# A causal mask added by VectorE with the row maximum, and mLSTM scores from three products of rounded halves

## The chip, the cores and the metric

One Trainium2 chip, one of its cores. The metric is the device time of one execution in microseconds (us); below are the times of three runs and the profile of one execution. PE is TensorE (matmuls; PEld is its weight load), DVE is VectorE, ACT is ScalarE, POOL is GpSimd, SP issues most DMAs.

## What is computed

A decoder of two layers over 256 tokens, width 2048, all in float32: an mLSTM layer with a gated ConvFFN, then a layer of differential attention with a gated ConvFFN, each on a residual stream, and a final RMSNorm. The change touches two places of it.

```python
# mLSTM, per head: scores of queries and keys, times a causal decay weight
s = jnp.einsum('bhtd,bhsd->bhts', qb, kb) * jnp.exp(dmat - m_t[..., None])
num = ... + jnp.einsum('bhts,bhsv->bhtv', s, vb)
...
# attention, per head and per each of its two score maps
s = jnp.einsum('bqhcd,bkhcd->bhcqk', qb, kb)
mask = (start + jnp.arange(Q_BLOCK))[:, None] >= jnp.arange(end)[None, :]
p = jax.nn.softmax(jnp.where(mask, s, -jnp.inf), axis=-1)
pd = p[:, :, 0] - lam * p[:, :, 1]
```

There are 8 heads in both; an mLSTM head has 128 query and key dimensions, an attention head two maps of 128.

## The kernel before

Weights stream from memory in tiles of 1 MB (`raw`, 4 buffers). `granule` takes half a tile and splits it for TensorE: ACT copies it, rounded to the format float32r, into a `w2` buffer (L376), and DVE puts what the rounding left beside it (L377). There are 5 `w2` buffers (`HL`). A matmul of two float32 operands is then three matmuls of halves, high by high, low by high and high by low. A matmul whose operands are plain float32 is run by TensorE as two instructions.

The mLSTM layer goes through q (`first_product`), the gates, k (`gemm`), v and the output gate o. For v and o (`gemm_tokens`, L437; four groups of 512 columns each) a granule is two of the 16 slices of the contraction, or 12 matmuls with 512 columns. In the two middle groups of o, `gemm_sevenths` (L503, L493) takes slices 8 to 11 in another way: `sevenths` loads one tile, DVE makes differences of its blocks (L449 to L451), and four `w2` buffers are filled from these (L458, L459). Their products go partly into the group's accumulators (`acc`), partly into two banks `mix`. A `w2` buffer comes free when the last product that reads it is done. The small PSUM banks (`small_ps`, 4 in all) are shared by `mix`, the scores, `val_ps`, `cols_ps` and others.

Work of a head is queued with `later(n, ...)`, to be written n granules on. When the two heads of a v group are ready, `weights(h)` forms the exponent of the decay in bank `w_ps` (L778), DVE adds the mask `mask_s` (L780), ACT takes the exponential (L782 to L784), PE the scores into `s_ps` (L786: 256 queries by the first 128 keys, L787: the last 128 by the last 128), DVE multiplies (L788), and the product is split (`split_weights`, L321, L323). Two granules later `values` multiplies it with v (`val_ps`, L335), squares (L343) and, later, `scaled` writes `hn` (L348). The heads' results are used when o's groups end (L819, L820, transposed at L357).

In attention, `halves(h)` splits keys and late queries into `kh, kl, qh, ql`. `softmax(h)` then forms, for each of the two maps, a bank `as_ps` with 384 columns: 256 for the later queries (L987, three products) and 128 for the first ones (L988, plain float32). One bfloat16 product of an identity with `mask_a` (L989) adds -1e30 above the diagonal. DVE takes the row maxima from the bank (L991, two a map), ACT the exponentials from the bank into `pc` (L996).

The order in which each engine gets its instructions is not that of the code: the framework (`schedule_with_timeline_sim`) places them by a timeline of its own, apart from `first_product`. Buffers of a pool are given out in that process too.

Of the kernel before, what the change touches and what calls it, by code (L numbers as in the profile page):

```python
# [10 lines left out]
F32 = mybir.dt.float32  # L11
F32R = mybir.dt.float32r
BF16 = mybir.dt.bfloat16
I32 = mybir.dt.int32
AF = mybir.ActivationFunctionType
ALU = mybir.AluOpType
AX = mybir.AxisListType
PSUM = bass.MemoryType.PSUM

P = 128  # L20
D = 2048
T = 256
# [11 lines left out]
SCALE = QK ** -0.5  # L34
LAMBDA_INIT = 0.8 - 0.6 * math.exp(-0.3)
NEG = -1e30
G = 512
NG = D // G
RAW = 4
# [29 lines left out]
def trunk(  # L69
# [6 lines left out]
    nc = tc.nc  # L76
    act, dve, pool, pe = nc.scalar, nc.vector, nc.gpsimd, nc.tensor

    const = ctx.enter_context(tc.tile_pool(name="const", bufs=1))
# [7 lines left out]
    def block(dt, name, width=T):  # L87

        b = big.tile([P, 2 * T + 4], dt, tag="block", name=name)
        return b[:, :width], b[:, width:2 * width], b[:, :2 * width]  # L90

    def tmp(name, rows=P, dt=F32):
        return work.tile([rows, T], dt, tag="tmp", name=name, bufs=8)

    def small_ps(name):
        return sm_ps.tile([P, 512], F32, tag="sm", name=name)
# [17 lines left out]
    def later(granules, fn):  # L114
        clock[1] += 1
        heapq.heappush(waiting, (clock[0] + granules, clock[1], fn))
# [21 lines left out]
    dve.tensor_copy(ident_r, ident)  # L138
    both_r = const.tile([P, HEADS], F32R, name="both_r")
    dve.tensor_tensor(both_r, ident[:, :HEADS], ident[:, 32:32 + HEADS], op=ALU.add)  # L140
    ident_b = const.tile([P, P], BF16, name="ident_b")
    make_identity(nc, ident_b)
    ones = const.tile([P, P], F32, name="ones")
    pool.memset(ones, 1.0)
    half_pi = const.tile([P, 1], F32, name="half_pi")
# [1 line left out]

    mask_a = const.tile([P, 2 * P], BF16, name="mask_a")
    mask_s = const.tile([P, 2 * P], BF16, name="mask_s")
    for m, sign in ((mask_a, 1), (mask_s, -1)):  # L150
        pool.memset(m, 0.0)
        m = m.rearrange("p (a c) -> p a c", a=2)
        pool.affine_select(out=m, in_=m, pattern=[[0, 2], [-sign, P]], compare_op=ALU.is_ge, fill=NEG, base=0, channel_multiplier=sign)

    def rows_of(ap):
        return ap.rearrange("(r c) -> r c", c=P)
# [55 lines left out]
    class Norm:  # L212
# [9 lines left out]
        def squares(self, g):  # L222
            for t in range(2):
                act.activation(tmp("sq").bitcast(BF16), stream[:, t, g * G:(g + 1) * G], AF.Square, accum_out=self.parts[:, t, g:g + 1])

# [78 lines left out]
    def scaled_split(ps, scale, name, width=T):  # L304
        h, l, hl = block(F32R, name, width)
        act.activation(h[:, :T], ps, AF.Identity, scale=scale)
        dve.scalar_tensor_tensor(l[:, :T], ps, scale, h[:, :T].bitcast(F32), op0=ALU.mult, op1=ALU.subtract)
        return h, l, hl
# [112 lines left out]

    def gemm_tokens(xs, w, col0, groups, evac, cw=G, lead=1):

        kn, hc = len(xs), WCOLS // cw // 2
        order, last = in_order(kn, hc, groups, lead, held=4 // hc)
        raws, accs = {}, {}
        for j, k0 in order:
            if k0 == 0:
                accs[j] = [acc_ps.tile([P, 2 * T], F32, tag="acc", name="acc")[:, :cw] for _ in range(2)]
            ps = accs[j]  # L430
            for i, (wh, wl) in enumerate(granule(w, col0 + j * cw, cw, k0, kn, raws, j)):
                k = k0 + i
                xh, xl, _ = xs[k]
                for t in range(2):
                    s = slice(t * P, (t + 1) * P)
                    for o, (a, b) in enumerate(((xh, wh), (xl, wh), (xh, wl))):
                        pe.matmul(ps[t], a[:, s], b, start=(k == 0 and o == 0), stop=(k == kn - 1 and o == 2))  # L437
            if k0 == last:
                evac(j, accs.pop(j))
            tick()  # L440

    def sevenths(w, c0, k0, n):


        raw = wpool.tile([P, 4, G], F32, tag="raw", name="raw", bufs=RAW)[:, :2 * n]
        loads.append(nc.sync.dma_start(raw, w[k0 * P:(k0 + 2 * n) * P, c0:c0 + G].rearrange("(k p) n -> p k n", p=P)))
        b = raw.rearrange("p (a k) (c n) -> p a (k c) n", a=n, c=2)
# [16 lines left out]
    def gemm_sevenths(xs, mixed, w, col0, groups, evac, at):  # L464
# [3 lines left out]
        for g in groups:  # L468
# [3 lines left out]
            while k0 < kn:  # L472
                if k0 in at:
                    if c is None:
                        c, d = small_ps("mix"), small_ps("mix")
                    parts = sevenths(w, col0 + g * G, k0, min(2, (kn - k0) // 2))
                    for p, (b1, b2, b3, t1, t3, t2, t4) in enumerate(parts):
# [200 lines left out]
    def mlstm(norm):  # L678
        xs = norm.sets[0]
        w = m_w_in[0]  # L680
        f = slice(32, 40)
# [69 lines left out]
        q, k, v, hn = ([None] * HEADS for _ in range(4))  # L751
# [13 lines left out]
        def evac_v(g, ps):  # L765
            for c in range(2):
                h = 2 * g + c
                v[h] = [scaled_split(ps[t][:, c * VD:(c + 1) * VD], norm.rt[:, t:t + 1], f"mv{h}_{t}", T + 2) for t in range(2)]
                for vh, vl, _ in v[h]:
                    pool.memset(vh[:, T:].bitcast(F32), 1.0)  # L770
                    pool.memset(vl[:, T:].bitcast(F32), 0.0)
                later(1 + 4 * c, lambda h=h: weights(h))

        def weights(h):

            wt = block(F32, "wt")[2][:, :384]
            w_ps = small_ps("w_ps")[:, :T]
            pe.matmul(w_ps, both_r[:, h:h + 1].broadcast_to([P, P]), rows["nm"], start=True, stop=True)  # L778
            diagonal = wt.rearrange("p (a c) -> p a c", c=P)[:, 0:3:2]
            dve.tensor_tensor(diagonal, w_ps.rearrange("p (a c) -> p a c", a=2), mask_s.rearrange("p (a c) -> p a c", a=2), op=ALU.add)  # L780
            c = rows["c"]
            act.activation(wt[:, P:T], w_ps[:, P:], AF.Exp, bias=c[:, h:h + 1])  # L782
            act.activation(wt[:, :P], wt[:, :P], AF.Exp, bias=c[:, h:h + 1])
            act.activation(wt[:, T:], wt[:, T:], AF.Exp, bias=c[:, 8 + h:9 + h])  # L784
            s_ps = small_ps("s_ps")
            pe.matmul(s_ps[:, :T], k[h][:, :P], q[h], start=True, stop=True)  # L786
            pe.matmul(s_ps[:, T:T + P], k[h][:, P:], q[h][:, P:], start=True, stop=True)  # L787
            dve.tensor_tensor(wt, s_ps[:, :384], wt, op=ALU.mult)  # L788
            p = split_weights(wt, h, "st")
            later(2, lambda: values(h, p))  # L790
# [148 lines left out]
    def attention(norm):  # L939
        (cos_t, sin_t), neg_lam = later_layers  # L940
        swap = list(range(16, 32)) + list(range(16))
        q, k, q_pairs = [None] * 2 * HEADS, [None] * 2 * HEADS, [None] * HEADS
# [34 lines left out]
        def softmax(h):  # L977
            nmax = work.tile([P, 4], F32, tag="nmax", name="nmax")
            l = work.tile([P, 4], F32, tag="l", name="l")
            p, halves = [], ((0, slice(0, T)), (1, slice(T, T + P)))  # L980
            for c in range(2):

                qc, kc = q[2 * h + c], k[2 * h + c]
                s_ps = small_ps("as_ps")
                qh, ql, kh, kl = wide[h][c]
                for o, (a, b) in enumerate(((qh, kh), (ql, kh), (qh, kl))):
                    pe.matmul(s_ps[:, :T], a, b, start=(o == 0), stop=False)  # L987
                pe.matmul(s_ps[:, T:T + P], qc[:, :P], kc[:, :P], start=False, stop=False)  # L988
                pe.matmul(s_ps[:, P:T + P], ident_b, mask_a, start=False, stop=True)  # L989
                for i, cs in halves:  # L990
                    dve.tensor_reduce(nmax[:, 2 * c + i:2 * c + i + 1], s_ps[:, cs], axis=AX.X, op=ALU.max)  # L991
                dve.tensor_scalar(nmax[:, 2 * c:2 * c + 2], nmax[:, 2 * c:2 * c + 2], -SCALE, None, op0=ALU.mult)
                pc = block(F32, "pc")[2][:, :384]
                for i, cs in halves:
                    a = slice(2 * c + i, 2 * c + i + 1)
                    act.activation(pc[:, cs], s_ps[:, cs], AF.Exp, bias=nmax[:, a], scale=SCALE, accum_out=l[:, a])  # L996
                p.append(pc)
            dve.reciprocal(l, l)
            dve.tensor_scalar(l[:, 2:4], l[:, 2:4], neg_lam, None, op0=ALU.mult)
            for i, cs in halves:  # L1000
                dve.tensor_scalar(p[1][:, cs], p[1][:, cs], l[:, 2 + i:3 + i], None, op0=ALU.mult)
                dve.scalar_tensor_tensor(p[0][:, cs], p[0][:, cs], l[:, i:i + 1], p[1][:, cs], op0=ALU.mult, op1=ALU.add)
            later(4, lambda: turned(h, p[0]))

        def turned(h, p):

            t_ps = small_ps("t_ps")
            for d, s in ((0, 2), (1, 0), (2, 1)):
                pe.transpose(t_ps[:, d * P:(d + 1) * P], p[:, s * P:(s + 1) * P], ident)
            pt[h] = split_weights(t_ps, h, "pt")  # L1010
# [162 lines left out]
```

## Time and profile before

| | us |
|---|---|
| median of three runs | 2247.79 (2247.59 to 2248.05) |
| span of the profiled execution, first to last instruction | 2246.0 |
| what lies between that span and the median | 1.8 |
| PE, DVE, ACT, POOL busy | 2236.4, 1800.5, 1297.7, 112.4 |
| mean granted clock of TensorE | 0.999 |

The profiled execution has no time of its own beside its span; taken at the median, 1.8 us lie around the span. Busy is the time in which an engine had at least one instruction under way. Matmuls overlap (a matmul with 512 columns lasts 0.39 us, and the next starts 0.23 us after it), so their cost is read from one start to the next and not from the duration.

### The profile page before, as it was taken

The page shows a single profiled execution, that of the slowest core. Times are in us where ns is not written, and L with a number is a line of the kernel's source. Part 1 is how long each engine was busy: PE and PEld are TensorE (multiplying, and loading weights), DVE is VectorE, ACT ScalarE, POOL GpSimd, SP SyncE. Part 2 cuts the span into 40 slices and gives each one's busy share as a digit, 9 for nine tenths or more (in the row PEclk, how much of TensorE's full clock was granted, in tenths as well). Part 3 has the DMA queues.
Part 4 walks back from the last instruction along what each step waited for, and adds up shares of the span by engine and source line. Part 5 has one row for each costly group of instructions (what it writes and reads, how often), then busy time and mean ns, then how long its engine had stood idle before and what let it go on. Part 6 is the DMA issues. An engine that isn't in the chain of part 4 may idle for free.

```text
span 2246.0 us, 33469 instructions
## 1 busy us (share of the span) xinstructions
PE 2236.4 (100%) x12847; PEld 1953.4 (87%) x12847; DVE 1800.5 (80%) x3007; ACT 1297.7 (58%) x2011; POOL 112.4 (5%) x275
## 2 busy tenths in 40 slices
PE   9999999999999999999999999999999999999998
PEld 9888888888888888888888888888888888888888
DVE  6756868787788877879998985677877988778896
ACT  5455655665554565656655655556565555556554
POOL 0014000000000000000022102300000000000000
PEclk9999999999999999999999999999999999999999
DMA  8554546555545755546566555465555457555464
GB/s 278 177 176 149 186 162 211 192 188 188 187 160 188 234 188 188 190 148 206 193 204 196 161 173 162 154 202 187 188 188 188 159 188 245 190 189 189 145 216 150
DMA packets 325636, 419.04 MB, mean 187 GB/s; under 512 B 9102, under 2 KB 238820, under 8 KB 325476
## 3 DMA queue, kind: packets, MB, share of 16 engines
q1 hardware_dynamic: 325444, 416.89, 56.7%
q8 instruction: 101, 1.65, 0.3%
q14 instruction: 59, 0.48, 0.1%
q10 hardware_dynamic: 32, 0.01, 0.0%
HBM read 414.77 MB, written 2.10 MB: 186 GB/s over the span
## 4 chain that ended last, share of the span: by engine, by line
PE 99%; DVE 0%; ACT 0%; issue 0%; DVEq 0%
PE acc L411 54%; PE acc L503 16%; PE acc L437 14%; PE mix L493 6%; PE acc L493 4%; PE acc L656 2%; PE val_ps L335 1%; PE acc L521 1%; PE turn_ps L231 0%; PE as_ps L987 0%; PE warm_ps L130 0%; PE turn_ps L637 0%; PE hn_ps L357 0%; PE gps L695 0%; PE as_ps L988 0%; PE an_ps L357 0%
## 5 line engine op out<-in xcount | busy, mean ns | idle before, releaser
L377 DVE TENSOR_TENSOR w<-raw,w 128x1024 fp32r<-128x1024 f32 x679 | 826.6, 1222 | 269.6 <-ACT w L376 267.3
L376 ACT ACTIVATE w<-raw 128x1024 fp32r<-128x1024 f32 x679 | 714.0, 1058 | 490.8 <-PE acc L411 322.8
L411 PE MATMUL acc<-x_f,w 128*128 128x512 f32 (+1 forms) x5632 | 987.5, 337 | 0.0
L411 PEld LDWEIGHTS acc<-x_f,w 128*128 128x128 f32 x5632 | 861.5, 188 | 122.8
L503 PE MATMUL acc<-w,hid 128*128 128x512 f32 x1080 | 268.1, 394 | 0.0
L503 PEld LDWEIGHTS acc<-w,hid 128*128 128x128 f32 x1080 | 195.3, 188 | 39.0
L411 PE MATMUL acc<-x_at,w 128*128 128x512 f32 (+1 forms) x1024 | 182.1, 338 | 0.0
L411 PEld LDWEIGHTS acc<-x_at,w 128*128 128x128 f32 x1024 | 156.6, 188 | 21.9 <-issue 0.2
L458 ACT ACTIVATE w<-diff 128x1024 fp32r<-128x1024 f32 x89 | 94.1, 1057 | 113.1 <-DVE diff L451 83.2
L417 ACT ACTIVATE low<-acc 128x256 f32<-128x256 f32 x216 | 78.9, 385 | 130.6 <-PE acc L411 127.7
L459 DVE TENSOR_TENSOR w<-diff,w 128x1024 fp32r<-128x1024 f32 x89 | 108.9, 1223 | 39.5 <-ACT w L458 39.1
L437 PE MATMUL acc<-w,x_a 128*128 128x512 f32 x576 | 138.0, 396 | 0.0
L437 PEld LDWEIGHTS acc<-w,x_a 128*128 128x128 f32 x576 | 106.8, 188 | 24.2
L493 PE MATMUL mix<-w,mix 128*128 128x256 f32 x801 | 119.4, 281 | 0.0
L418 DVE TENSOR_TENSOR acc<-acc,low 128x256 f32<-128x256 f32 x216 | 84.3, 430 | 38.4 <-ACT low L417 38.0
L493 PEld LDWEIGHTS mix<-w,mix 128*128 128x128 f32 x801 | 107.1, 188 | 2.4 <-DVE w L459 0.2
L863 ACT ACTIVATE c<-u,conv 128x256 f32<-128x256 f32 x176 | 98.2, 593 | 5.9 <-DVE u L861 5.6
L458 ACT ACTIVATE w<-raw 128x768 fp32r<-128x768 f32 x89 | 74.7, 840 | 36.7 <-PE acc L503 22.8
L968 POOL TENSOR_TENSOR sw<-sw,sin_t 32x256 f32<-32x256 f32 x32 | 39.1, 1235 | 1076.9 <-DVE sw L967 1026.4
L437 PE MATMUL acc<-w,x_at 128*128 128x512 f32 x384 | 91.4, 395 | 0.0
L459 DVE TENSOR_TENSOR w<-raw,w 128x768 fp32r<-128x768 f32 x89 | 84.9, 953 | 2.5 <-ACT w L458 2.3
L493 PE MATMUL acc<-w,hid 128*128 128x256 f32 x450 | 86.3, 281 | 0.0
(318 smaller groups left out, 2343.8 us busy)
## 6 DMA issues: line engine op xcount, KB each, us to landing
raw<-in_w_up_dram SPq DMA_DIRECT2D x176, 1024.0 KB
raw<-in_w_down_dram SPq DMA_DIRECT2D x79, 1024.0 KB
raw<-in_m_w_in_dram SPq DMA_DIRECT2D x46, 1024.0 KB
raw<-in_w_kv_dram SPq DMA_DIRECT2D x32, 1024.0 KB
raw<-in_m_w_out_dram SPq DMA_DIRECT2D x16, 1024.0 KB
raw<-in_w_q_dram SPq DMA_DIRECT2D x16, 1024.0 KB
raw<-in_w_o_dram SPq DMA_DIRECT2D x16, 1024.0 KB
raw<-in_w_down_dram SPq DMA_DIRECT2D x15, 512.0 KB
```

The costliest lines, as they stand in the source:

```text
L376: act.activation(w2[:, :hc, 0], part, AF.Copy)
L377: dve.tensor_tensor(w2[:, :hc, 1], part, w2[:, :hc, 0].bitcast(F32), op=ALU.subtract)
L411: pe.matmul(to, a, b, start=(k == 0 and o == 0), stop=(k == kn - 1 and o == len(ops) - 1))
L417: act.activation(low, p[:, T:], AF.Copy)
L418: dve.tensor_tensor(p[:, :T], p[:, :T], low, op=ALU.add)
L437: pe.matmul(ps[t], a[:, s], b, start=(k == 0 and o == 0), stop=(k == kn - 1 and o == 2))
L458: act.activation(w2[:, :m, 0], src, AF.Copy)
L459: dve.tensor_tensor(w2[:, :m, 1], src, w2[:, :m, 0].bitcast(F32), op=ALU.subtract)
L493: pe.matmul(to, u, v, start=start and o == 0, stop=end and o == 2 and to is not a and to is not b, skip_group_check=True)
L503: pe.matmul(ps, u[:, s], v, start=(k0 + i == 0 and o == 0), stop=(k0 + i == kn - 1 and o == 2), skip_group_check=True)
L656: pe.matmul(ps[j], a, b, start=(k == 0 and o == 0 and j % 2 == 0), stop=(k == KD - 1 and o == 2), skip_group_check=True)
L863: act.activation(c, u, AF.Identity, bias=cw[:, 3, f:f + 1], scale=cw[:, 2, f:f + 1])
```

## The change

In attention, the product with the identity goes, with its identity and its weight load. DVE's `tensor_tensor_reduce` adds `mask_a` to the scores as it reads them from the bank, writes the sum to `pc` and takes its maximum in the same instruction; ACT reads the exponent's argument from `pc`, no longer from the bank. `mask_a` now masks its second 128 columns alone.

In mLSTM, a new step `scores(h)` rounds and splits the head's k and q (256 columns each) into four tiles of the pool `tmp` (8 buffers), by two ACT copies and two DVE subtractions. The scores are then three products of halves for each of their two parts.

```diff
+LOWEST = -3e38
...
-    ident_b = const.tile([P, P], BF16, name="ident_b")
-    make_identity(nc, ident_b)
...
-    for m, sign in ((mask_a, 1), (mask_s, -1)):
+    for m, sign, ones_of in ((mask_a, 1, slice(1, 2)), (mask_s, -1, slice(0, 2))):
...
+                later(4 * c, lambda h=h: scores(h))
                 later(1 + 4 * c, lambda h=h: weights(h))
+        parts = {}
+        def scores(h):
+            parts[h] = []
+            for value, name in ((k[h], "k"), (q[h], "q")):
+                hi, low = tmp(f"m{name}h", dt=F32R), tmp(f"m{name}l", dt=F32R)
+                act.activation(hi, value, AF.Copy)
+                dve.tensor_tensor(low, value, hi.bitcast(F32), op=ALU.subtract)
+                parts[h] += [hi, low]
...
-            pe.matmul(s_ps[:, :T], k[h][:, :P], q[h], start=True, stop=True)
-            pe.matmul(s_ps[:, T:T + P], k[h][:, P:], q[h][:, P:], start=True, stop=True)
+            kh, kl, qh, ql = parts.pop(h)
+            for to, a, b in ((slice(0, T), slice(0, P), slice(0, T)), (slice(T, T + P), slice(P, T), slice(P, T))):
+                for o, (u, v) in enumerate(((kh, qh), (kh, ql), (kl, qh))):
+                    pe.matmul(s_ps[:, to], u[:, a], v[:, b], start=(o == 0), stop=(o == 2))
...
-                pe.matmul(s_ps[:, T:T + P], qc[:, :P], kc[:, :P], start=False, stop=False)
-                pe.matmul(s_ps[:, P:T + P], ident_b, mask_a, start=False, stop=True)
-                for i, cs in halves:
-                    dve.tensor_reduce(nmax[:, 2 * c + i:2 * c + i + 1], s_ps[:, cs], axis=AX.X, op=ALU.max)
-                dve.tensor_scalar(nmax[:, 2 * c:2 * c + 2], nmax[:, 2 * c:2 * c + 2], -SCALE, None, op0=ALU.mult)
+                pe.matmul(s_ps[:, T:T + P], qc[:, :P], kc[:, :P], start=False, stop=True)
                 pc = block(F32, "pc")[2][:, :384]
                 for i, cs in halves:
+                    dve.tensor_tensor_reduce(pc[:, cs], s_ps[:, cs], mask_a[:, i * P:], 1.0, LOWEST, ALU.add, ALU.max, nmax[:, 2 * c + i:2 * c + i + 1])
+                dve.tensor_scalar(nmax[:, 2 * c:2 * c + 2], nmax[:, 2 * c:2 * c + 2], -SCALE, None, op0=ALU.mult)
+                for i, cs in halves:
                     a = slice(2 * c + i, 2 * c + i + 1)
-                    act.activation(pc[:, cs], s_ps[:, cs], AF.Exp, bias=nmax[:, a], scale=SCALE, accum_out=l[:, a])
+                    act.activation(pc[:, cs], pc[:, cs], AF.Exp, bias=nmax[:, a], scale=SCALE, accum_out=l[:, a])
```

Since the framework orders the instructions, the order moves in other places too, in the v and o groups above all. Line numbers of the changed kernel differ a little from those of the profile before.

The first place is PE's row at the scores of head 0. Before:

```order
L778 MATMUL w_ps<-nm,both_r 128x256
L786 MATMUL s_ps<-mq_775,mk_932 128x256
L787 MATMUL s_ps<-mq_775,mk_932 128x128
L437 MATMUL acc<-w_1413,x_a_185 128x512 x6
L437 MATMUL acc<-w_1413,x_a_193 128x512 x6
```

Now, at the same place:

```order
L789 MATMUL w_ps<-nm,both_r 128x256
L800 MATMUL s_ps<-mqh,mkh 128x256
L800 MATMUL s_ps<-mql,mkh 128x256
L800 MATMUL s_ps<-mqh,mkl 128x256
L800 MATMUL s_ps<-mqh,mkh 128x128
L800 MATMUL s_ps<-mql,mkh 128x128
L800 MATMUL s_ps<-mqh,mkl 128x128
L436 MATMUL acc<-w_1420,x_a_180 128x512 x6
```

Two plain products became six of halves. For heads 1 to 7 the scores also stand later: head 7's were in o's group 0 and now stand in the middle of o's group 1.

The second place is PE's row where o's group 1 ends (accumulators `acc_2573`, `acc_2574` before; `acc_2664`, `acc_2665` now) and group 2 begins (`acc_2856`, `acc_2857` now). The numbers of `w2` count buffers as they are given out. `sevenths` filled `w2_2657` to `w2_2666` before and fills `w2_2748` to `w2_2757` now, four buffers in each. Before, from the last granule but one of group 1 to its last, `w2_2728`, which comes behind these rows:

```order
L503 MATMUL acc_2573<-w2_2713,x_a_13_549 128x512 x3
L503 MATMUL acc_2574<-w2_2713,x_a_13_549 128x512 x3
L931 MATMUL lam_ps_2595<-pr_2592,ones_123 128x2
L493 MATMUL mix_2649<-w2_2657,x_a_8_399 128x256 x3
L493 MATMUL mix_2649<-w2_2660,mix_2268 128x256
L493 MATMUL mix_2649<-w2_2660,mix_2269 128x256
L493 MATMUL mix_2649<-w2_2660,mix_2268 128x256
L493 MATMUL mix_2649<-w2_2663,x_a_10_471 128x256 x3
L493 MATMUL mix_2649<-w2_2666,mix_2281 128x256
L493 MATMUL mix_2649<-w2_2666,mix_2282 128x256
```

Now, first between the last two granules of group 1, `w2_2804` and `w2_2819` (`cols_ps` are transposes of convolution parameters, `val_ps_2544` the values of head 7):

```order
L502 MATMUL acc_2664<-w2_2804,x_a_13_544 128x512 x3
L1077 MATMUL cols_ps_2532<-ident_109,conv_rows0_2301 128x88
L1077 MATMUL cols_ps_2535<-ident_109,conv_rows0_2301 128x88
L1077 MATMUL cols_ps_2538<-ident_109,conv_rows0_2302 128x88
L1077 MATMUL cols_ps_2541<-ident_109,conv_rows0_2302 128x88
L334 MATMUL val_ps_2544<-mv7_0_2259,st7_2491 128x258 x3
L502 MATMUL acc_2664<-w2_2819,x_a_14_625 128x512
```

then between `w2_2819` and the first granule of group 2, `w2_2860`:

```order
L502 MATMUL acc_2664<-w2_2819,x_a_15_631 128x512 x3
L502 MATMUL acc_2665<-w2_2819,x_a_15_631 128x512 x3
L1077 MATMUL cols_ps_2606<-ident_109,conv_rows1_2308 128x88
L1077 MATMUL cols_ps_2609<-ident_109,conv_rows1_2308 128x88
L502 MATMUL acc_2856<-w2_2860,x_a_0_180 128x512 x2
L502 MATMUL acc_2857<-w2_2860,x_a_0_180 128x512 x2
```

and between `w2_2860` and the next, `w2_2897`:

```order
L502 MATMUL acc_2856<-w2_2860,x_a_1_188 128x512 x3
L502 MATMUL acc_2857<-w2_2860,x_a_1_188 128x512 x3
L502 MATMUL acc_2856<-w2_2897,x_a_2_237 128x512 x2
L502 MATMUL acc_2857<-w2_2897,x_a_2_237 128x512 x2
L944 MATMUL lam_ps_2686<-pr_2683,ones_118 128x2
L492 MATMUL mix_2740<-w2_2748,x_a_8_394 128x256 x3
L492 MATMUL mix_2740<-w2_2751,mix_2347 128x256
```

The products into `mix`, the last to read the four buffers of `sevenths`, stood inside group 1, ahead of its last granule. They now stand in group 2, behind the first products of its second granule.

The third place is ACT's row there. Before:

```order
L819 ACTIVATE o_2536<-acc_2285,rt_half_151 128x256
L819 ACTIVATE o_2539<-acc_2286,rt_half_151 128x256
L819 ACTIVATE o_2542<-acc_2285,rt_half_151 128x256
L819 ACTIVATE o_2545<-acc_2286,rt_half_151 128x256
L376 ACTIVATE w2_2713<-raw_2711 128x2x512
L348 ACTIVATE hn7_2548<-val_ps_2453,yh_2479 128x256
L348 ACTIVATE hn7_2548<-val_ps_2457,yh_2479 128x256
L306 ACTIVATE mo0_2556<-hn_ps_2551,half_h_145 128x256
L376 ACTIVATE w2_2728<-raw_2711 128x2x512
```

Now:

```order
L375 ACTIVATE w2_2819<-raw_2802 128x2x512
L347 ACTIVATE hn6_2496<-val_ps_2398,yh_2424 128x256
L347 ACTIVATE hn6_2496<-val_ps_2402,yh_2424 128x256
L342 ACTIVATE sq_2556,ms_2555<-val_ps_2544 128x256
L342 ACTIVATE sq_2558,ms_2555<-val_ps_2548 128x256
L832 ACTIVATE o_2627<-acc_2364,rt_half_146 128x256
L832 ACTIVATE o_2630<-acc_2365,rt_half_146 128x256
L832 ACTIVATE o_2633<-acc_2364,rt_half_146 128x256
L832 ACTIVATE o_2636<-acc_2365,rt_half_146 128x256
L375 ACTIVATE w2_2860<-raw_2858 128x2x512
L375 ACTIVATE w2_2897<-raw_2858 128x2x512
L347 ACTIVATE hn7_2639<-val_ps_2544,yh_2570 128x256
```

Heads 6 and 7 are finished (`hn6`, `hn7`) later against the granules: `hn7` stood ahead of the copy for the last granule of group 1, and now stands behind those for the first two granules of group 2.

More of the change, by code (lines that the diff above doesn't have):

```diff
@@ L149, in trunk @@
     mask_s = const.tile([P, 2 * P], BF16, name="mask_s")
-    for m, sign in ((mask_a, 1), (mask_s, -1)):
+    for m, sign, ones_of in ((mask_a, 1, slice(1, 2)), (mask_s, -1, slice(0, 2))):
         pool.memset(m, 0.0)
-        m = m.rearrange("p (a c) -> p a c", a=2)
-        pool.affine_select(out=m, in_=m, pattern=[[0, 2], [-sign, P]], compare_op=ALU.is_ge, fill=NEG, base=0, channel_multiplier=sign)
+        m = m.rearrange("p (a c) -> p a c", a=2)[:, ones_of]
+        pool.affine_select(out=m, in_=m, pattern=[[0, m.shape[1]], [-sign, P]], compare_op=ALU.is_ge, fill=NEG, base=0, channel_multiplier=sign)
     def rows_of(ap):
```

## The prediction

> **What bounds the kernel now.** I read the page's first lines and its chain first, then the costliest groups, then stretches of the three places that the change touches, and then PE's timeline there.
>
> ```profile
> span 2246.0 us, 33469 instructions
> PE 2236.4 (100%) x12847; PEld 1953.4 (87%) x12847; DVE 1800.5 (80%) x3007; ACT 1297.7 (58%) x2011; POOL 112.4 (5%) x275
> PE 99%; DVE 0%; ACT 0%; issue 0%; DVEq 0%
> L377 DVE TENSOR_TENSOR w<-raw,w 128x1024 fp32r<-128x1024 f32 x679 | 826.6, 1222 | 269.6 <-ACT w L376 267.3
> L376 ACT ACTIVATE w<-raw 128x1024 fp32r<-128x1024 f32 x679 | 714.0, 1058 | 490.8 <-PE acc L411 322.8
> ```
>
> PE is busy for 2236.4 of 2246.0 us and is 99% of the chain that ended last. A microsecond of PE's starts taken away is one gained, and a microsecond in which PE waits is one lost. DVE's 80% counts only where it makes PE wait. The last two rows are the two halves of a granule: 1.06 us of ACT, then 1.22 us of DVE.
>
> The same by stretch. Columns: start:end and length; then sum of busy time (and instructions) of PE, PEld, DVE, ACT and POOL; then granted clock, DMA share and GB/s. The stretches are the mLSTM scores of all heads, o's groups 1 and 2, and attention's softmax.
>
> ```profile
> 120.00:235.00 115.00, 115.00 (x540) 95.07 (x539) 76.84 (x166) 69.67 (x137) 33.96 (x114) 1.00 0.49 155
> 235.00:265.00 30.00, 29.73 (x164) 25.19 (x163) 24.54 (x61) 17.70 (x33) 0.00 (x0) 1.00 0.50 172
> 1235.00:1345.00 110.00, 110.00 (x633) 95.69 (x632) 100.58 (x238) 63.49 (x142) 12.91 (x14) 1.00 0.53 168
> ```
>
> PE has no idle time in the first and the third, and 0.27 us in the second. DVE has 38 us free in the first but only 9.4 in the third.
>
> **The change part by part.** *The masks.* PE in attention, around one map (start, duration, engine and line, tiles; x is how many in one row):
>
> ```profile
> 1236.09 0.28 PE L987 MATMUL as_ps<-kh,qh 128*128 128x256 f32 x1
> ...
> 1236.56 0.86 PE L411 MATMUL acc<-x_at,w 128*128 128x512 f32 x4
> 1237.38 0.39 PE L988 MATMUL as_ps<-ak,aq 128*128 128x128 f32 x2
> 1237.60 0.27 PE L989 MATMUL as_ps<-mask_a,ident_b 128*128 128x256 bf16 x1
> 1237.63 0.36 PE L987 MATMUL as_ps<-kl,qh 128*128 128x256 f32 x1
> 1237.83 0.39 PE L988 MATMUL as_ps<-ak,aq 128*128 128x128 f32 x2
> ```
>
> Four products with 256 columns fill 1236.09 to 1236.56, so each costs 0.118 us from start to start. From the mask's start to the next L988, 0.23 us hold the mask and one such product: the mask costs 0.11. There are 8 heads with two maps: 16 x 0.11 = 1.8 us less on PE. The mask's durations of 0.27 us would give 4.3, but durations of matmuls overlap.
>
> *The mLSTM scores.* Before, with the 512-column products around them:
>
> ```profile
> 126.02 2.03 PE L437 MATMUL acc<-w,x_a 128*128 128x512 f32 x8
> 127.88 0.28 PE L778 MATMUL w_ps<-nm,both_r 128*128 128x256 f32 x1
> 128.00 0.59 PE L786 MATMUL s_ps<-mq,mk 128*128 128x256 f32 x2
> 128.43 0.38 PE L787 MATMUL s_ps<-mq,mk 128*128 128x128 f32 x2
> ```
>
> Eight products take 127.88 - 126.02 = 1.86 us, 0.232 each. The plain 256-column product (two instructions) takes 128.43 - 128.00 = 0.43; the 128-column one takes 0.22 in attention (1237.38 to 1237.60). Together 0.65 a head. In their place stand three halves' products with 256 columns, 3 x 0.118 = 0.35, and three with 128. For halves' products as narrow as that the nearest rows are these:
>
> ```profile
> 46.60 0.23 PE L294 MATMUL spread_ps<-ident_r,sp_h 128*128 128x128 f32 x1
> 46.66 0.28 PE L295 MATMUL spread_ps<-ident_r,sp_l 128*128 128x128 f32 x1
> 46.78 0.27 PE L294 MATMUL spread_ps<-ident_r,sp_h 128*128 128x128 f32 x1
> 46.89 0.27 PE L295 MATMUL spread_ps<-ident_r,sp_l 128*128 128x128 f32 x1
> 47.00 0.69 PE L656 MATMUL acc<-x_a,w 128*128 128x256 f32 x4
> ```
>
> The steps are 0.06, 0.12, 0.11 and 0.11. I take 0.11, as three of four do: half the columns cost about as much as 256. So 0.35 + 0.33 = 0.68 a head, 0.03 more than before, and +0.3 us over 8 heads. At 0.06 for each it is 0.53 a head, -1.0 us; at the 0.215 of one of L786's two instructions for all of the narrow ones it is 1.0, +2.8 us.
>
> The Trainium skill speaks against the 0.11: its page "TensorE: Matmul & The Clock Gate", section "Back-to-back issue gap", makes the gap proportional to the columns, some 56 ns at 128 and 109 at 256. By it the new scores would be an estimated 0.50 us a head, 1.2 us less over the heads, and the total 2248.8. The same page's section on LDWEIGHTS gives the load of 128 rows some 107 ns, and three of the four steps look like that load and not like the columns.
>
> *The splits ahead of the scores* are two ACT copies and two DVE subtractions a head, like these of the same shape:
>
> ```profile
> L300 ACT ACTIVATE hid<-c x88: 396/402/420, 424.1 to 2130.3; 128x256 fp32r<-128x256 f32 x88
> L301 DVE TENSOR_TENSOR hid<-c,hid x88: 415/419/425, 425.8 to 2132.9; 128x256 fp32r<-128x256 f32 x88
> ```
>
> That is 0.80 us of ACT and 0.84 of DVE a head, 6.4 and 6.7 us in all, beside the 45 and 38 us that the two have free in the first stretch. I take nothing for them. Without that cover a head would cost up to 1.6 us.
>
> *What the order moves.* By front's second place the four `w2` buffers of `sevenths` are now read last in group 2, behind the first products of `w2_2897`. There are five buffers. So `w2_2804`, `w2_2819`, `w2_2860` and `w2_2897` must share the one that is left, and each copy can begin only when PE has done the last product of the granule ahead. Before, three granules shared one buffer too, but PE had the `mix` products and transposes to do meanwhile:
>
> ```profile
> 242.68 0.88 PE L335 MATMUL val_ps<-mv,st 128*128 128x258 f32 x6
> 243.40 0.32 PE L1065 MATMUL cols_ps<-ident,conv_rows 88*128 88x88 f32 x2
> 243.51 0.48 PE L503 MATMUL acc<-w,x_a 128*128 128x512 f32 x1
> ...
> 246.52 0.66 PE L357 MATMUL hn_ps<-ident,o 128*128 128x128 f32 x4 [0.27 <-DVE conv L1066]
> ...
> 248.29 2.11 PE L503 MATMUL acc<-w,x_a 128*128 128x512 f32 x8
> 250.24 0.28 PE L931 MATMUL lam_ps<-pr,ones 128*128 128x2 f32 x2
> 250.39 0.62 PE L493 MATMUL mix<-w,x_a 128*128 128x256 f32 x3
> 251.90 1.10 PE L503 MATMUL acc<-w,x_a 128*128 128x512 f32 x4
> ```
>
> ACT at the same place:
>
> ```profile
> 250.22 0.48 ACT L306 ACTIVATE mo<-hn_ps,half_h 128x256 fp32r<-128x256 f32 x1
> 250.58 1.07 ACT L376 ACTIVATE w<-raw 128x1024 fp32r<-128x1024 f32 x1
> ```
>
> The granule's last product ended at 248.29 + 2.11 = 250.40, the copy into the same buffer began at 250.58 and ended at 251.65, and PE started on it at 251.90. PE had gone on to other work at 250.24. So a hand-over needs a cover from 250.24 to 251.65 at least, 1.41 us, and to 251.90 at most, 1.66; as PE waited for nothing here, I take a value near the lower end, 1.45. Now, between `w2_2804` and `w2_2819`, PE has four `cols_ps` transposes (0.11 a pair by the rows of 243.40 and 243.51, so 0.22) and three products `val_ps` (six took 0.72, so 0.36): 0.58, lacking 0.87. Between `w2_2819` and `w2_2860` one pair, 0.11, lacking 1.34. Between `w2_2860` and `w2_2897` nothing, lacking 1.45. Together 3.7 us. DVE's low halves (1.22 each, behind the copies) have only the high products ahead of them, four to eight at 0.23, and DVE also empties the `cols_ps` banks between the transposes: 0 to 2 us, and I take 0.8, nearer the lower end since most of the 1.22 us is covered. What PE lost here before, the 0.27 in the row of 246.52 and about as much around it, 0.5, goes. So +4.0 us. The lower end is 0, if the copy's order in time differs from what the count says; the upper one is under the rivals. Behind the late buffer the next granule is late as well, and nothing else: the weights' transfers wait for `raw`, which is free earlier than PE needs it.
>
> *The row maxima* become sums with maxima, on the same columns. The rows of each kind, least, mean and most ns:
>
> ```profile
> L991 DVE TENSOR_REDUCE nmax<-as_ps x32: 267/344/425, 1237.9 to 1342.5; 128x1 f32<-128x256 f32 x16, 128x1 f32<-128x128 f32 x16
> L780 DVE TENSOR_TENSOR wt<-w_ps,mask_s x8: 400/420/426, 129.0 to 233.4; 128x256 f32<-128x256 f32 x8
> L996 ACT ACTIVATION_READ_ACCUMULATOR pc<-as_ps,nmax x32: 189/202/216, 1242.0 to 1344.6; 128x1 f32 x32
> ```
>
> A 256-wide sum from a bank costs what a 256-wide maximum does, about 0.42, so I take nothing. The fused instruction has no row before. A cheaper one gains nothing, since PE does not wait for it; a dearer one may take DVE's free 9.4 us, 0.29 us for each of 32. ACT reads `pc` in place of the bank, with the same shapes: nothing, ACT has 46 us free there.
>
> The sum is -1.8 + 0.3 + 4.0 = +2.5: a span of 2248.5 against 2246.0, and with the 1.8 us around it 2250.3 against the median of 2247.79.
>
> **The rivals.** *The hand-overs are covered*, since ACT and DVE fetch ahead where I count one buffer, and only PE's own work counts: -1.5, 2246.3. For it: PE waited 0.27 us in the whole second stretch before, with one buffer for three granules. Against it: the work that covered them has moved behind.
>
> *Slower by more than the measurement tells: each hand-over pays both halves.* If DVE is behind by then (24.5 of 30 us busy in the second stretch, the splits on top), PE waits for 1.45 + 1.22 us three times, less the cover of 0.7 and the 0.5 that goes: +6.8, net +5.3, 2253.1. It decides from 6.0 us of waits on (6.0 - 1.5 = 4.5). Against it: the high products go first.
>
> *DVE becomes the bound in attention.* If the fused instruction is dear, beyond the 0.29 us of room DVE falls behind: at 0.8 us more each, 32 x 0.8 - 9.4 = 16 us, of which the granules that DVE has finished ahead of PE take a part between nothing and all; with half, +8, 2258. The nearest row for a dear one is ACT's: handing out its accumulated sum takes 0.20 us by itself (L996), still below 0.29. The Trainium skill, "VectorE: DVE Perf Modes", section "Two Vector instructions with no wait between them", counts an op that also writes its accumulator as two instructions, which points the same way; no run here shows it yet for DVE.
>
> **How the numbers follow.** This kernel's measurement tells 0.2%, 4.5 us, from no change: 2243.3 to 2252.3 is the same. My case, waits of 2 to 5.5 us, has 0.62: the buffers count out, and the pieces of the cover are rows. Covered hand-overs have 0.17, both halves paid 0.14, DVE as the bound 0.05, and a gain beyond 4.5 us, for which I see no source, 0.02. The low end, 2246.0, takes in the covered case, with its scores a little cheaper; the high end, 2252.8, is my case with 6.5 us of waits, or with the dear narrow products. Faster 0.02, same 0.79, slower 0.19.
>
> **What would show it.** In the profile after, right: L989's kind gone, with 16 instructions less on PE in attention and no new waits there; six `s_ps` products that take 0.68 us a head from the first start to the next work; PE waits in rows of `acc` at o's groups 1 to 2, released by ACT's or DVE's `w`, adding up to 3 to 5 us; the fused instruction within 0.3 us of 0.42 at 256 columns. Wrong: no waits at the boundary, or far more; narrow steps of 0.06; PE waiting in attention for DVE; or a new wait in another place, which the order was not read for.

## The result: 2253.2 us against 2247.6, 0.25% slower, and the profile after

The changed kernel takes 2253.23 us (median of 9 runs, 2252.69 to 2254.38) against 2247.57 (9 runs, 2247.39 to 2248.05): a ratio of 1.0025, 95% interval 1.0017 to 1.0033. The forecast was 2250.3, with a range up to 2252.8: slower, but less so, and the time lies 0.4 us above the range.

The first lines of the page and its chain:

```profile
span 2251.3 us, 33525 instructions
PE 2235.5 (99%) x12847; PEld 1951.8 (87%) x12847; DVE 1806.3 (80%) x3055; ACT 1301.7 (58%) x2027; POOL 113.8 (5%) x273
PE 98%; DVE 1%; ACT 0%; POOL 0%; DMA 0%; issue 0%; DVEq 0%; SPq 0%; ACTq 0%
```

The span is 5.3 us longer and PE is busy for 0.9 us less. So PE waits where it did not, and the list of its waits says for whom (engine, line, releaser: us in total, times, longest):

```profile
PE acc L502 <- ACT w L375: 2.1, 2, 1.1
PE acc L410 <- DVE ak L978: 1.8, 2, 1.0
PE acc L436 <- DVE ak L978: 0.9, 1, 0.9
PE val_ps L334 <- DVE conv L1078: 0.6, 1, 0.6
PE an_ps L356 <- ACT nrm L347: 0.6, 1, 0.6
PE cols_ps L1077 <- DVE conv L1078: 0.3, 1, 0.3
```

Left out are a wait of 1.0 us at the start, which was there before, and one of 0.3 at the first granule of q. Three of the rows lie in o's groups 1 and 2 (`w`, and `conv` twice), where waits were forecast. The other three lie in attention, where none were. The same by stretch, the columns as in the prediction:

```profile
235.00:265.00 30.00, 26.95 (x154) 22.53 (x153) 26.50 (x85) 21.53 (x44) 0.00 (x0) 1.00 0.32 106
1235.00:1345.00 110.00, 107.32 (x606) 92.61 (x605) 99.43 (x258) 62.61 (x133) 17.59 (x14) 1.00 0.51 164
```

PE is idle for 3.05 us in the first stretch (0.27 before) and for 2.68 in the second (none before). DVE in attention is no busier than it was: 99.43 us against 100.58.

**The border of o's groups**, on PE and then on ACT:

```profile
247.00 0.32 PE L1077 MATMUL cols_ps<-ident,conv_rows 88*128 88x88 f32 x2
247.58 0.45 PE L1077 MATMUL cols_ps<-ident,conv_rows 88*128 88x88 f32 x2 [0.27 <-DVE conv L1078]
248.67 0.60 PE L334 MATMUL val_ps<-mv,st 128*128 128x258 f32 x3 [0.63 <-DVE conv L1078]
...
250.85 2.12 PE L502 MATMUL acc<-w,x_a 128*128 128x512 f32 x8
252.81 0.32 PE L1077 MATMUL cols_ps<-ident,conv_rows 88*128 88x88 f32 x2
254.12 1.20 PE L502 MATMUL acc<-w,x_a 128*128 128x512 f32 x4 [0.99 <-ACT w L375]
...
255.94 2.11 PE L502 MATMUL acc<-w,x_a 128*128 128x512 f32 x8
259.20 1.21 PE L502 MATMUL acc<-w,x_a 128*128 128x512 f32 x4 [1.15 <-ACT w L375]
```

```profile
247.40 1.04 ACT L375 ACTIVATE w<-raw 128x1024 fp32r<-128x1024 f32 x1
253.01 1.06 ACT L375 ACTIVATE w<-raw 128x1024 fp32r<-128x1024 f32 x1 [0.82 <-PE acc L502]
258.09 1.06 ACT L375 ACTIVATE w<-raw 128x1024 fp32r<-128x1024 f32 x1 [4.02 <-PE acc L502]
```

The last two rows with a wait for `w` are hand-overs as forecast. A granule's last product ends at 252.97 (250.85 + 2.12); ACT, idle until then, copies from 253.01 to 254.07; PE goes on at 254.12. The same at 258.05, 258.09, 259.15 and 259.20. From start to start, beyond a product's own 0.23 or a transpose's 0.055, these two cost 1.18 and 1.31 us. At the first of the three places, ahead of them, PE waits for something else: DVE has to empty the banks of the transposes `cols_ps` (L1078), and that costs 0.45 + 0.87.

**Attention**, at the border between two key groups, PE and then DVE:

```profile
1288.28 0.38 PE L1001 MATMUL as_ps<-ak,aq 128*128 128x128 f32 x2
1288.42 0.94 PE L410 MATMUL acc<-x_at,w 128*128 128x512 f32 x4
1290.34 1.85 PE L410 MATMUL acc<-x_at,w 128*128 128x512 f32 x9 [0.97 <-DVE ak L978]
```

```profile
1288.12 0.42 DVE L1004 CUSTOM_DVE_ANT_0 pc<-as_ps,mask_a 128x256 f32<-128x256 f32 x1 [0.62 <-PE as_ps L1001]
...
1289.77 0.75 DVE L978 TENSOR_TENSOR ak<-acc,rstd_at 128x256 f32<-128x256 f32 x2
```

`ak` empties the banks of the key group before, which the next group needs. In DVE's order it stands behind the four fused instructions of a head, and these wait for PE's score products, which PE now runs as late as four products ahead of that next group (five at the next two borders). So PE waits for DVE, which has waited for PE. Before, the order on DVE was the same, but the score products stood in the middle of the group. DVE and then PE at the same head, before:

```profile
1280.71 1.15 DVE L991 TENSOR_REDUCE nmax<-as_ps 128x1 f32<-128x256 f32 x4
1281.98 0.75 DVE L965 TENSOR_TENSOR ak<-acc,rstd_at 128x256 f32<-128x256 f32 x2
1280.88 8.49 PE L411 MATMUL acc<-x_at,w 128*128 128x512 f32 x47
```

By the order, 38 of these 47 products still belong to the old group, some 6.6 us of work, and `ak` is done 1.85 us after the first of them. PE's rows in the order for the head after that one, before:

```
L987 MATMUL as_ps_12563<-kl_12493,qh_12494 128x256
L988 MATMUL as_ps_12563<-ak4_12456,aq4_11435 128x128
L989 MATMUL as_ps_12563<-mask_a_127,ident_b_118 128x256
L411 MATMUL acc_12620<-x_at_9_11451,w2_12671 128x256
```

and now, at that head's last scores:

```
L1000 MATMUL as_ps_12645<-kl_12576,qh_12577 128x256
L1001 MATMUL as_ps_12645<-ak4_12539,aq4_11526 128x128
L410 MATMUL acc_12701<-x_at_14_11860,w2_12811 128x256
```

They stood behind slice 9 of the group's 16 (counted from 0) and stand in slice 14 now. This happens at three borders; `an_ps`, after the last, waits for results of a head that come late from ACT.

### The profile page after: what moved, and what is told of

Same layout as the page of the kernel before. It is cut to its first block, busy times and chain, and to the rows that moved or that the text cites. A ratio compares the mean times of both kernels' runs of the same rounds, so it can differ in the third digit from the quotient of the medians.

```text
span 2251.3 us, 33525 instructions
## 1 busy us (share of the span) xinstructions
PE 2235.5 (99%) x12847; PEld 1951.8 (87%) x12847; DVE 1806.3 (80%) x3055; ACT 1301.7 (58%) x2027; POOL 113.8 (5%) x273
## 4 chain that ended last, share of the span: by engine, by line
PE 98%; DVE 1%; ACT 0%; POOL 0%; DMA 0%; issue 0%; DVEq 0%; SPq 0%; ACTq 0%
PE acc L410 54%; PE acc L502 16%; PE acc L436 13%; PE mix L492 6%; PE acc L492 4%; PE acc L655 2%; PE val_ps L334 1%; PE acc L520 1%; PE turn_ps L230 0%; PE s_ps L800 0%; PE as_ps L1000 0%; DMA raw<-in_m_w_in_dram 0%; PE gps L694 0%; PE hn_ps L356 0%; DVE pc L1004 0%; PE an_ps L356 0%
## 5 line engine op out<-in xcount | busy, mean ns | idle before, releaser
L981 POOL TENSOR_TENSOR sw<-sw,sin_t 32x256 f32<-32x256 f32 x32 | 43.7, 1383 | 1063.4 <-DVE sw L980 1046.2
L436 PEld LDWEIGHTS acc<-w,x_at 128*128 128x128 f32 x384 | 71.5, 188 | 17.3 <-PE acc L410 1.1
```

## The experiments

Theory A is the reading above: two orders that changed, each with waits of its own. Its rivals are a dear fused instruction (B, a rival of the prediction too), a late effect of o's delay in attention (C), and in o the work of the splits. The table has two stretches of each trace. Kernels that share the code and order of a stretch agree in it to 0.3 us. The first runs from the first product of v to the first of mLSTM's output projection and holds scores and o; the second from attention's first product to that of the second ConvFFN. Starts are taken from PE's rows, in us; "later" is the end of the trace against that of before. Medians are of 11 runs, that of the change of 9, that of e5 of 5; e10 and e11 are one run each.

| kernel | median us | first stretch | second stretch | later |
|---|---|---|---|---|
| before | 2247.57 | 196.43 | 384.29 | 0 |
| the change | 2253.23 | 200.46 | 386.57 | 5.3 |
| e1 mask alone | 2251.60 | 196.60 | 386.77 | 3.0 |
| e2 scores alone | 2253.05 | 200.48 | 384.09 | 5.3 |
| e3 scores sooner | 2249.22 | 196.26 | 386.68 | 1.4 |
| e4 both moved | 2244.75 | 196.25 | 382.36 | -3.4 |
| e5 plain maxima, late | 2264.62 | 196.41 | 397.74 | 14.8 |
| e6 plain scores, late | 2250.31 | 200.17 | 384.34 | 2.3 |
| e7 scores alone, sooner | 2246.72 | 196.36 | 384.29 | -0.5 |
| e8 mask alone, later | 2245.32 | 196.55 | 382.34 | -2.6 |
| e9 softmax later | 2248.87 | 200.48 | 382.39 | 1.1 |
| e10 as e2 | 2252.04 | 200.48 | 384.07 | 4.3 |
| e11 as e7 | 2246.35 | 196.25 | 384.31 | -1.4 |

The kernel before had medians of 2247.80 to 2247.86 beside the experiments.

**e1, the mask alone.** `scores(h)` is left out and the two plain score products are put back.

> The attention half of the change alone; the mLSTM scores stay two plain products. Theory A (the order): the fused instruction costs DVE no more than the maximum did, but the framework now puts a map's score products at the end of a key group, and DVE empties the group's banks only behind the row maxima that wait for these products; three waits of PE for ak, 3.1 us with their borders, plus 0.75 at an_ps, against 1.8 for the masks and 0.65 at the start: +1.4, about 2249.0. Theory B (the price): the fused instruction is dear and DVE falls behind; the same three waits, and longer DVE instructions. Theory C: the waits in attention are a late effect of o's delay in mLSTM; then they are gone here, and the kernel is 2.4 faster than before, 2245.1. Under A and B nothing is lost in o's groups.

2251.60 us, 1.0016 of before (1.0007 to 1.0024). PE's waits are the same three for `ak` and the one for `an_ps`; o's stretch is as before. Theory C is out. The loss of 3.7 us is larger than the 1.4 forecast. The second stretch is 2.5 us longer, against 2.1 by the sum. The rest lies where nothing was changed: 0.4 us are gained ahead of the first stretch in place of 0.65, 0.65 are lost behind the second, and 2.5 us lie around the span, against 1.8 in the other kernels (2.2 in e8).

**e2, the scores alone.** Attention as before, the mLSTM half of the diff kept.

> The mLSTM half alone; attention keeps its mask product and its plain maxima. Theory A: four granules through one buffer at the border of o's groups 1 and 2 cost 3.6 to 3.9 us here as they do in the whole change, the scores themselves nothing (0.65 us a head before and after), and attention has no wait for ak: 2251.3. If the masks' edit had a share in the waits of o, less: 2248 to 2250.

2253.05 us, 1.0021 (1.0013 to 1.0030), 1.75 above what theory A gave. The first stretch is 4.05 us longer, to 0.02 us what the whole change shows there, and attention has no wait. Elsewhere 2.2 us are gained up to the end of the second stretch and 3.45 lost behind it. There a weight tile landed late for DVE. DVE worked on without a pause for 18 us, and then PE waited for what came of it; DVE's timeline and PE's list of waits:

```profile
2180.08 1.23 DVE L449 TENSOR_TENSOR diff<-raw 128x1024 f32<-128x1024 f32 x1 [2.30 <-DMA raw<-in_w_down_dram]
```

```profile
PE mix L493 <- ACT w L458: 1.1, 1, 1.1
```

With a second wait, 0.5 for DVE's `w`, that is 1.6 of the 3.45 us; the other 1.8 have no wait beside them.

**e3, the scores sooner.** The whole change, with

```diff
-                later(4 * c, lambda h=h: scores(h))
-                later(1 + 4 * c, lambda h=h: weights(h))
+                later(2 * c, lambda h=h: scores(h))
+                later(2 * c, lambda h=h: weights(h))
```

> The whole change, but the splits and the weights of the second head of a pair are queued two granules after its group, not four and five, and those of the first at once. By the order no granule of o then has to wait for a buffer (cover at least 1.6 us everywhere). Theory A (one buffer): o's waits go, 3.6 to 3.9 us less than the whole change: 2249.4. Rival: the waits come from the work of the splits on ACT and DVE, which is all still there: 2253.

2249.22 us, 1.0005 (0.9997 to 1.0014), 4.0 below the whole change, with every split still there. O's waits are gone and its stretch is 0.2 us shorter than before; the waits for `ak` are all there. The splits' work is not the cause.

**e4, both moved.** As e3, and

```diff
-                    later(4, lambda: then(j))
+                    later(6, lambda: then(j))
```

> As the one before, and in attention the softmax of a head is queued six granules after its key group, not four: the score products then stand at least 3 us of PE work ahead of the next group. Theory A: the waits for ak go as well, 3.1 us: 2246.3, which is 1.2 below the kernel before. Theory B (the fused instruction is dear, DVE is behind): the waits come back at another place of attention, 2249.4 as the run before.

2244.75 us, 0.9985 (0.9976 to 0.9994): faster than before by 3.1 us, and 1.6 below what theory A gave. Of these 1.6, 1.2 lie in the second stretch, which is 4.3 us shorter than in e3: the wait at `an_ps`, which the 3.1 left out, went as well. The list of PE's waits in e4 has a single row, at the start:

```profile
PE warm_ps L131 <- DVE warm L127: 1.1, 1, 1.1
```

In attention PE is busy throughout, and DVE carries the same fused instructions with 9.0 us free:

```profile
1235.00:1345.00 110.00, 110.00 (x626) 95.65 (x626) 101.00 (x280) 67.24 (x149) 16.73 (x14) 1.00 0.53 168
```

Theory B is out: at the same price the waits are gone.

**e5, plain maxima, late.** The kernel before, with its mask products and maxima, and the one edit `later(4, lambda: then(j))` to `later(2, ...)`.

> The kernel before, with its mask product and its plain maxima; the one edit is that a head's softmax is queued two granules after its key group, not four. In the order the score products of four heads then end 0.0 to 0.1 us of PE work ahead of the next key group. Theory A (the order makes the waits, not the instruction): from a map's last score product to the end of ak it takes some 1.8 us, so four waits of PE for ak of about 1.7 to 1.8: +7, about 2254.8. Theory B (the price of the fused instruction makes them): no fused instruction here, no wait: 2247.8.

2264.62 us, 1.0076 (1.0062 to 1.0090). With no fused instruction in it, PE waits for `ak` at four borders:

```profile
PE acc L411 <- DVE ak L965: 6.1, 3, 2.5
PE acc L437 <- DVE ak L965: 1.2, 1, 1.2
PE val_ps L335 <- ACT av L306: 1.7, 1, 1.7
```

7.3 us for `ak`, 7 forecast. That agreement is partly luck: the four are 2.5, 1.2, 2.4 and 1.2, where 1.7 to 1.8 each were expected. The time missed by 10 us. From start to start the four cost 8.3. The third row and one of 0.9 for DVE's `av`, at attention's v, cost 2.9, which was read from no order ahead. Right behind these two waits the granted clock is 0.5 for 3.4 us (1374.2 to 1377.6; 0.57 in the stretch from 1374 to 1378), products with 512 columns start 0.43 us apart there in place of 0.23, and that costs some 1.6. Another 1.8 are lost behind the second stretch, and the median lies 2.0 above the run of the trace: the mean granted clock of e5's runs is 0.996 to 0.998, against 0.999 before. The mechanism stands, the total was not foreseen.

**e6, plain scores, late.** The kernel before, with `later(1 + 4 * c, ... weights(h))` made `later(3 + 4 * c, ...)`: no splits, but by the order four granules through one buffer.

> The kernel before, with its plain scores and no splits; the one edit is that a head's decay weights are queued two granules later. By the order four granules then share one w2 buffer at the border of o's groups 1 and 2, with 0.28, 0.88 and 0.22 us of PE work between them. Theory A (a hand-over needs 1.45 us of cover): PE waits 1.17 + 0.57 + 1.23 = 3.0 us there, less the 0.45 that it waited before: +2.5, about 2250.3. Rival (the work of the splits makes the waits): 2247.8.

2250.31 us, 1.0011 (1.0002 to 1.0020), as forecast, though not in each part. The second and third hand-over cost 0.68 and 1.23 us from start to start (0.57 and 1.23 expected). At the first, PE waits for the banks of transposes and not for the copy: that costs 1.0 (1.17 expected), and 0.5 more at a transpose ahead of it. The first stretch is 3.7 us longer, against 2.5 expected, and 1.5 us are gained ahead of it and behind it, where nothing was changed: the agreement of the total is partly luck. PE's waits there, but for one of 0.3 at a transpose:

```profile
PE acc L503 <- ACT w L376: 1.4, 2, 1.1
PE cols_ps L1065 <- DVE conv L1066: 0.5, 2, 0.3
```

So four granules through one buffer give PE's wait for the copy without the change's splits or scores.

**e7, the scores alone, sooner.** e2 with the edit of e3.

> The mLSTM half alone, with the sooner queueing of e3. Theory A: the scores cost PE what they cost before (0.65 us a head), the hand-overs in o are covered, the 0.45 us wait of before is gone: 2247.0 to 2247.5 against 2247.8, no difference that shows.

2246.72 us, 0.9995 (0.9987 to 1.0004): no difference that can be told. The first stretch is 0.1 us shorter than before (0.2 in e11), though the wait of 0.45 at o's border is gone: three passes in place of two plain products save nothing and cost PE some 0.25 (below).

**e8, the mask alone, later.** e1 with the edit of e4.

> The attention half alone, with the softmax queued six granules after its key group. Theory A: no wait for ak, and the masks' 16 products are saved, 1.8 to 1.9 us, with 0.4 to 0.65 at the start: 2245.4. Theory B (dear instruction): waits of PE in attention at another place, about 2248 or above.

2245.32 us, 0.9989 (0.9981 to 0.9998). The second stretch is 1.95 us shorter than before: the 16 masks, 1.8 forecast.

**e9, the softmax later.** The whole change with the second edit of e4 alone.

> The whole change with the one edit in attention: the softmax of a head queued six granules after its key group; o's groups as in the whole change. Theory A: the three waits for ak and the one at an_ps go, 4.2 us less than the whole change, o's 3.9 us of waits stay: 2249.0. If the waits in attention followed from o's delay, they would stay: 2253.

2248.87 us, 4.4 below the whole change, 1.0005 (0.9996 to 1.0014). The first stretch keeps its 200.48 us, the second has the masks' gain. The two losses are independent: e3 takes away one, e9 the other, e4 both.

**e10 and e11, e2 and e7 once more.**

> e2 once more, for its profile. In e2 a weight tile landed 2.3 us late near 2180 us and PE lost 1.7 us there. If that is chance, it is gone here and the kernel ends about 3.5 us later than the one before (span 2249.5); if it comes with this edit, it is there again (span 2251.3).

> e7 once more, for its profile. There too a tile landed 1.3 us late near 2174 us, and PE lost 1.1 us. By chance: gone, span 2244.4. With the edit: again there, span 2245.4.

In both the late tile is there again, with shorter waits (0.9 and 1.0 us on DVE, 0.7 on PE in each): spans of 2250.3 and 2244.6, against 2251.3 and 2245.4. The stretches repeat to 0.1 us. So it isn't mere chance, and goes with these two programs: in the traces of the whole change, e3, e4 and e9, PE has no wait there. Why the scores' edit alone brings it stays open.

## Why the prediction missed

**The step that failed** is "The row maxima become sums with maxima", taken at nothing. Its prices were right. Three of a head's four fused instructions in DVE's timeline after:

```profile
1302.80 0.28 DVE L1004 CUSTOM_DVE_ANT_0 pc<-as_ps,mask_a 128x128 f32<-128x128 f32 x1
1303.01 0.09 DVE L1004 DVE_READ_ACCUMULATOR2_ANT nmax<- 128x1 f32 x1
1303.01 0.42 DVE L1004 CUSTOM_DVE_ANT_0 pc<-as_ps,mask_a 128x256 f32<-128x256 f32 x1
1303.35 0.09 DVE L1004 DVE_READ_ACCUMULATOR2_ANT nmax<- 128x1 f32 x1
1303.35 0.29 DVE L1004 CUSTOM_DVE_ANT_0 pc<-as_ps,mask_a 128x128 f32<-128x128 f32 x1
1303.56 0.09 DVE L1004 DVE_READ_ACCUMULATOR2_ANT nmax<- 128x1 f32 x1
```

From start to start, 0.34 us at 256 columns and 0.21 at 128; the plain maxima of before take 0.33 and 0.20. The durations of all 32, least, middle and most ns, are like those of L991 in the prediction:

```profile
L1004 DVE CUSTOM_DVE_ANT_0 pc<-as_ps,mask_a x32: 279/352/425, 1240.3 to 1348.5; 128x256 f32<-128x256 f32 x16, 128x128 f32<-128x128 f32 x16
```

The accumulator's read, 0.09, starts together with the next instruction and costs nothing to be seen. The Trainium skill, "VectorE: DVE Perf Modes", section "Two Vector instructions with no wait between them", says that an op which writes out its accumulator is two instructions; the rows agree, and that did not make it dear. What was not read is the order in attention: the section on the order looked for moved work in mLSTM alone, and attention was named only as a place for a dear instruction. "PE waiting in attention for DVE" stands among the prediction's own signs of being wrong. The wait goes by way of banks that DVE empties, not through DVE's load. From start to start, beyond the products' own, the four waits cost 1.14 + 1.01 + 1.01 + 0.71 = 3.9 us; the second stretch is 4.2 us longer in the whole change than in e4 and e9. Whether the fused instruction or the missing mask product made the framework put the scores later was not tried by itself.

**The hand-overs in o**, forecast at 3.7 + 0.8 - 0.5 = +4.0, came in at +3.4: 1.18 for the second (1.34 forecast), 1.31 for the third (1.45), 0.45 + 0.87 at the first, less the 0.45 of before. The second and third are the mechanism of the prediction, with a cover of 1.3 us needed and not 1.45. The first is not: PE was forecast to wait 0.87 there for ACT's copy, but that copy ended at 248.44 and PE was let go on at 248.67: both waits are for the banks of the transposes, for which the prediction had a part of its 0.8. No wait is for DVE's low halves, the rest of the 0.8. The first stretch is 4.03 us longer; beside the +3.4 it holds the scores and some 0.4 in slower steps, half of it in the first products behind waits. That this comes so near to 4.0 is partly luck. e3 and e6 show both directions of the hand-overs.

**The masks**, -1.8: e8 and e9 show -1.9.

**The scores**, +0.3 with steps of 0.11. The rows of head 7:

```profile
242.88 0.28 PE L800 MATMUL s_ps<-mqh,mkh 128*128 128x256 f32 x1
242.99 0.28 PE L800 MATMUL s_ps<-mql,mkh 128*128 128x256 f32 x1
243.11 0.28 PE L800 MATMUL s_ps<-mqh,mkl 128*128 128x256 f32 x1
243.23 0.22 PE L800 MATMUL s_ps<-mqh,mkh 128*128 128x128 f32 x1
243.29 0.28 PE L800 MATMUL s_ps<-mql,mkh 128*128 128x128 f32 x1
243.40 0.27 PE L800 MATMUL s_ps<-mqh,mkl 128*128 128x128 f32 x1
243.51 0.68 PE L502 MATMUL acc<-w,x_a 128*128 128x512 f32 x2
```

The narrow steps are 0.06, 0.11 and 0.11, and a head takes 0.63 us up to the next product. Before it took 0.57, from 128.00 to this row:

```profile
128.57 1.17 PE L437 MATMUL acc<-w,x_a 128*128 128x512 f32 x4
```

The 512-column product behind the scores takes longer than its 0.23, however: by 0.05 us now and by 0.08 before. With that it is 0.69 against 0.66 a head, or +0.25 over the eight heads, close to the forecast. Of the narrow products only the first is quick; the others start 0.11 apart, as TensorE's weight loads do there (at 243.23, 243.34 and 243.45; a load is 128 by 128 here, so that the prediction's 128 rows are 128 columns as well). The Trainium skill's formula in "TensorE: Matmul & The Clock Gate", section "Back-to-back issue gap", given there for an isolated product, fits that first step alone (56 ns, 61 measured); the same section gives 81 ns for a stream with weight loads, where these three average 94, which is what counts here.

**The rival that gave 2253.1** (both halves paid) has the right time and the wrong cause: PE's waits in o are for ACT's copy and for banks of transposes, as the rows say, none is for DVE's half of a granule, and they come to +3.4, not to +6.8.

**Elsewhere** the whole change gains 0.7 us up to the first v product and 0.9 between the two stretches, and loses 0.6 after them. Between the stretches the kernels differ by up to 1.5 us, though PE's order in the ConvFFN there, which fills most of that time, is the same in all of them by the tiles' names. Of what makes it, the runs show only that it repeats with the program (e2 and e10: 819.58 and 819.59 us between the stretches, 821.03 before) and goes with the mLSTM half of it: 821.0 to 821.1 where that is as before (e1, e5, e8), 820.4 to 820.5 with the scores sooner (e3, e4, e7, e11), 819.6 in e2, e9 and e10, and 820.1 in the whole change.

So -1.9 for the masks, +4.0 for the scores and o together, +4.2 for attention and -1.0 elsewhere make the 5.3 us of the two traces, where -1.8, +0.3 and +4.0 had made 2.5. The 4.2 in attention is more than the whole miss of 2.8 between the two sums; the gains elsewhere, which nothing foresaw, hid a part of it.

## What to carry to other kernels

When an edit lets a framework order the instructions anew, read the new order at every place where a buffer or a bank passes from one user to the next, not only in the stage where the largest rows moved: for each, the work that the bound engine has between the last use and the next. A hand-over costs what it takes from the last use to the next (1.3 us here, for a copy of 1.06), less that work. Where this was read ahead it gave the waits for a copy within 0.2 us each, and the single waits for `ak` in e5 within about 0.8. An edit whose work is worth a few microseconds can be undone by its order: here two edits of how many granules later a step is queued are worth 8.5 us, and turned a loss of 5.7 us into a gain of 3.1.

## What the runs showed of the hardware

- DVE's fused sum and maximum out of a bank into SBUF takes nearly as long as the maximum alone (from start to start 0.34 us against 0.33 at 256 columns, 0.21 against 0.20 at 128), and its accumulator's read of 0.08 to 0.09 us overlaps the next instruction.
- Narrow products of halves behind one another start 0.11 us apart, as their weight loads do, except the first behind a wide one (0.06).
- The work between the two stretches took up to 0.2% less time from program to program (819.6 to 821.1 us), and the same again when a program was repeated.
- In e5 the granted clock fell to 0.5 for 3.4 us right behind two waits of PE, 1.7 and 0.9 us long; inside a program this was seen once, and the waits of up to 2.5 us in the same trace had no such drop behind them.
